# The running sums of squares of the norms added by the vector engine instead of GpSimd

## The chip, the cores and the metric

The kernel runs on one core of one Trainium2 chip. The core has a matrix engine (TensorE, PE in the profile), a vector engine (VectorE, DVE), a scalar engine (ScalarE, ACT), a general engine (GpSimd, POOL) and a queue that issues DMAs (SyncE, SP). The metric is the time of one execution on the device in microseconds (us), as a median of several runs. Outputs are float32.

## The reference, cut to what matters

A two-layer encoder trunk takes 1024 frames of a new stream and 32 frames of a running one, with a model width of 1024. Layer 0 mixes by a gated linear recurrence with 8 heads, layer 1 by sliding-window attention with a sink; each mixer is followed by a gated feed-forward network (FFN) of width 2816. Every sub-layer has a norm in front of it and one behind it, and the result is added to the residual:

```
def rms_norm(x, w):
    xf = x.astype(F32)
    y = xf * lax.rsqrt(jnp.mean(xf * xf, axis=-1, keepdims=True) + NORM_EPS)
    return (y * w.astype(F32)).astype(x.dtype)
...
        x = x + rms_norm(mix, norm_mix_post[layer])
        hf = rms_norm(x, norm_ffn_pre[layer])
        a, b = jnp.split(hf @ w_ffn_in[layer], 2, axis=-1)
        x = x + rms_norm((jax.nn.silu(a) * b) @ w_ffn_out[layer], norm_ffn_post[layer])
```

The change concerns the mean of squares in `rms_norm`: a sum over 1024 features for each of the 1056 frames.

## The kernel before, in words

Activations lie with features on the 128 partitions and frames along the free dimension. The 1056 frames are cut into three blocks, b = 0, 1, 2, of 384, 384 and 288 frames, and the 1024 features into eight slices, k = 0 to 7. Each float32 product on TensorE is made of three products of a high and a low part: weights are split into `wh` (ScalarE casts, L102 or L98) and `wl` (VectorE subtracts, L103 or L99), activations into `xh` (ScalarE, L217 or L220) and `xl` (VectorE, L218 or L221).

A norm needs the sum of squares over all eight slices of a block. `sq_acc` (L176 on) is called once for each slice. For the first slice ScalarE squares straight into the accumulator `acc` (L178). For each of the other seven, ScalarE squares into a scratch tile `tmp` (L181; four buffers that many places share) and the square is added to `acc` (L182). `rnorm` (L184 on) then multiplies a 128x128 matrix of ones with `acc` on TensorE (L188), which sums over the partitions, and VectorE and ScalarE make the inverse square root of it by turns (L163 to L171, with squares and linear steps at L191 and L192).

The sums stand at four places: when the input is loaded (`xload`), behind each mixer's output projection (`outproj`), behind each FFN's last product (`ffn`, L592 adds the product to `mix` and `sq_acc` follows), and in `postnorm`, which scales a slice (L251), adds the residual `xo` that a DMA loaded (L252), splits it into `xh` and `xl`, and sums the squares for the next norm. Eight norms of three blocks with seven adds each give 168 adds.

Around them, the first mixer makes the decays of its recurrence: VectorE makes products of queries and decays (L821 to L851), GpSimd products of keys and decays (L816, L817, L833 to L835, L855 to L858, L941, L942). The second mixer rotates queries and keys: VectorE multiplies (L1129 to L1132), GpSimd combines (L1133, L1134).

The program is written through a framework that fixes, before the run, the order of the instructions of each engine; on the chip each engine takes its instructions in that order and waits at semaphores for what they need. `rnorm` and `rcol` place their small matmuls behind the last dense product that was written so far (`after_dense`), so that their place in TensorE's order is nearly fixed. What one engine has in its queue behind a waiting instruction waits too.

Of the kernel before, what the change touches and what calls it, by code (L numbers as in the profile page):

```python
# [59 lines left out]
def build(nc, tc, I, O):  # L60
    ctx = ExitStack()
    mult, add, sub, mn = ALU.mult, ALU.add, ALU.subtract, ALU.min
# [20 lines left out]
    def tmp(bufs=4):  # L83
        return tp.tile([128, 384], F32, tag="tmp", name="tmp", bufs=bufs)
# [91 lines left out]
    def sq_acc(acc, W, src, first):  # L176
        if first:
            nc.scalar.activation(acc[:, :W], src, AF.Square)  # L178
        else:
            q = tmp()  # L180
            nc.scalar.activation(q[:, :W], src, AF.Square)  # L181
            nc.gpsimd.tensor_tensor(acc[:, :W], acc[:, :W], q[:, :W], add)  # L182

    def rnorm(acc, dst, W, ps=None):  # L184

# [37 lines left out]
    def postnorm(b, mix, acc, w2, xold, wnext, spill, yout, done, more=None, full=None):  # L223
# [25 lines left out]
        for k in range(KT):  # L249
            m = mix[:, k, :]  # L250
            nc.vector.scalar_tensor_tensor(m, m, pcol(w2, k), rb2[:, :W], mult, mult)  # L251
            nc.vector.tensor_tensor(m, m, xos[k][:, :W], add)  # L252
            load()
            if yout is None:
                if full is None:
                    put_x(b, k, m, xs, wnext)
                sq_acc(nacc, W, m, k == 0)
            if k % 2:
                nc.sync.dma_start(dst[:, k - 1:k + 1, :], mix[:, k - 1:k + 1, :])
                if k < KT - 1:  # L260
                    yield
# [23 lines left out]
    def ffn(L, nx, post1, post, wmix, v1, w2, xold, wnext, spill, yout, res):  # L285
# [286 lines left out]
        for b in range(NB):  # L572
            W = BL[b][1]
            pss, un = {}, {}
            accs[b] = newacc(b)

            def first(k):
                if k % 2 == 0:
                    un[0] = units()
                pss[k] = mmps()  # L580
                fmul(pss[k], 2, b, un[0], k % 2, True, False)

            for k in range(4 if b == 0 else 0):
                first(k)
            for k in range(KT):
                if k not in pss:
                    first(k)
                fmul(pss[k], 3, b, units(), 0, False, True)
                if k == 1 and b + 1 < NB:
                    gload(3, b + 1)  # L590
                d = dst(k, b)
                nc.vector.tensor_tensor(d, d, pss[k][:, :W], add)  # L592
                sq_acc(accs[b], W, d, k == 0)
                if b > 0:
                    for _ in range(steps[b][k]):
                        step(b - 1)
# [53 lines left out]
    def outproj(b, arr, pre, w2, xold, wnext, spill, ahead=None):  # L650

        W = BL[b][1]
        oh, ol = os[b]
        mix = mbt[b] = mbs[b].tile([128, KT, 384], F32, tag=mtag(b), name="mixb", bufs=1)
        acc = newacc(b)
        for k in range(KT):
            if k % 2 == 0:
                units = wpair(arr, k // 2, scale=pre)
                if ahead and k < KT - 2:
                    wahead(arr, k // 2 + 1, scale=pre)  # L660
                elif ahead:
                    wahead(*ahead)
            ps = mmps()
            mm_fm(ps, W, units, (k % 2) * 128, lambda q: oh[:, q, :], lambda q: ol[:, q, :])
            nc.scalar.copy(mix[:, k, :W], ps[:, :W])
            sq_acc(acc, W, mix[:, k, :W], k == 0)
            yield

        def done(*r):
            nx[b] = r  # L670

        yield from postnorm(b, mix[:, :, :W], acc, w2, xold[b], wnext, spill[b], None, done,
                            full=("back", "here", None)[b])
# [840 lines left out]
```

## Time and profile before

| what | value |
|---|---|
| median of 3 runs | 2544.05 us (2542.91 to 2549.28) |
| the profiled execution | 2548.6 us |
| its span, first to last instruction | 2546.8 us |
| mean granted TensorE clock in the span | 0.988 |

The durations that the prediction uses come from the profiled execution, which took 2548.6 us; 1.8 us of it lie outside the span. A row of the timeline gives the start in us from the span's start, the length in us, engine, source line, operation, the tile written and those read, shapes, how many instructions the row merges, and in square brackets for how long the engine was idle before and what released it. PEld is TensorE's loading of weights, which runs beside its matmuls.

### The profile page before, as it was taken

The numbers are of one execution on the slowest core, as the hardware profiler recorded it, in microseconds if no ns is written. First come the engines' busy times: TensorE is split into PE (matmuls) and PEld (weight loads), VectorE is DVE, ScalarE is ACT, GpSimd is POOL, SyncE is SP. The second block draws the span as 40 slices with busy tenths as digits, with TensorE's granted clock in tenths as the row PEclk, the third lists the DMA queues.
The fourth block names the chain that finished last, engine by engine and source line by source line (L and its number), as shares of the span: only waits on it lengthen the run. The fifth ranks groups of instructions, "written<-read, shape, count | busy, mean of one in ns | idle before, by whom it ended". The sixth has DMA issues, their size and how long they took to land.

```text
span 2546.8 us, 44040 instructions
## 1 busy us (share of the span) xinstructions
PE 2469.6 (97%) x17124; PEld 2373.7 (93%) x17124; DVE 1722.0 (68%) x3510; ACT 1101.2 (43%) x2395; POOL 457.5 (18%) x644
## 2 busy tenths in 40 slices
PE   7999998999999999999998999999999999999997
PEld 7999998998899999999998997777999999999997
DVE  8788789888776666643467747787776666652456
ACT  6555565666533333341344424565533333342333
POOL 4443444332300000000033321121300000000012
PEclk9999999999999999999999999998999999999998
DMA  5233334343422222242445542332422222252455
GB/s 171 91 101 99 115 110 138 124 135 107 156 72 82 80 77 76 78 166 77 150 158 165 181 128 63 86 120 70 162 80 76 76 76 77 77 177 76 147 168 156
DMA packets 124153, 287.98 MB, mean 113 GB/s; under 512 B 13432, under 2 KB 68632, under 8 KB 123944
## 3 DMA queue, kind: packets, MB, share of 16 engines
q1 hardware_dynamic: 123944, 285.17, 34.9%
q8 instruction: 134, 2.20, 0.3%
q14 instruction: 75, 0.61, 0.1%
HBM read 237.25 MB, written 48.07 MB: 112 GB/s over the span
## 4 chain that ended last, share of the span: by engine, by line
PE 74%; DVE 12%; DMA 5%; ACT 4%; issue 3%; POOL 1%; SPq 0%; POOLq 0%; DVEq 0%; ACTq 0%
PE mm L141 23%; PE mm L507 18%; PE mm L416 14%; PE c L416 6%; PE mm L153 5%; DVE wl L103 2%; PE sc L1272 2%; PE pav L1330 1%; ACT wh L102 1%; PE ptp L1312 1%; DVE wl L99 1%; DMA wst<-in_wfq 1%; DMA xl<-g 1%; DVE mixb L252 1%; DMA xo<-in_x 1%
## 5 line engine op out<-in xcount | busy, mean ns | idle before, releaser
L141 PE MATMUL mm<-xh,wh 128*128 128x384 f32 (+1 forms) x1968 | 632.9, 322 | 11.1 <-ACT xh L220 7.5
L141 PE MATMUL mm<-xh,wl 128*128 128x384 f32 (+1 forms) x1968 | 624.3, 317 | 5.5 <-DVE wl L99 3.0
L141 PE MATMUL mm<-xl,wh 128*128 128x384 f32 (+1 forms) x1968 | 627.1, 319 | 2.0 <-DVE xl L221 1.3
L182 POOL TENSOR_TENSOR acc<-acc,tmp 128x384 f32<-128x384 f32 (+1 forms) x168 | 211.3, 1262 | 1693.7 <-ACT tmp L181 1669.4
L103 DVE TENSOR_TENSOR wl<-wst,wh 128x1024 fp32r<-128x1024 f32 (+1 forms) x301 | 379.3, 1264 | 145.0 <-ACT wh L102 144.4
L102 ACT CAST wh<-wst 128x1024 fp32r<-128x1024 f32 (+1 forms) x301 | 313.6, 1046 | 343.5 <-PE mm L507 198.9
L141 PEld LDWEIGHTS mm<-xh,wh 128*128 128x128 f32 x1968 | 372.8, 190 | 20.9 <-ACT xh L220 7.5
L141 PEld LDWEIGHTS mm<-xh,wl 128*128 128x128 f32 x1968 | 373.0, 190 | 13.8 <-issue 5.6
L141 PEld LDWEIGHTS mm<-xl,wh 128*128 128x128 f32 x1968 | 372.6, 189 | 13.2 <-issue 4.7
L507 PE MATMUL mm<-xh,wl 128*128 128x384 f32 (+1 forms) x768 | 247.1, 322 | 4.7 <-DVE wl L103 4.7
L507 PE MATMUL mm<-xh,wh 128*128 128x384 f32 (+1 forms) x768 | 247.1, 322 | 0.0
L507 PE MATMUL mm<-xl,wh 128*128 128x384 f32 (+1 forms) x768 | 247.0, 322 | 0.0
L153 PE MATMUL mm<-wh,xh 128*128 128x256 f32 (+1 forms) x648 | 189.1, 292 | 3.2 <-DVE tmp L1130 2.2
L153 PE MATMUL mm<-wh,xl 128*128 128x256 f32 (+1 forms) x648 | 185.0, 285 | 0.0
L153 PE MATMUL mm<-wl,xh 128*128 128x256 f32 (+1 forms) x648 | 184.6, 285 | 0.0
L400 ACT CAST sh<-sr 128x512 fp32r<-128x512 f32 x144 | 89.5, 622 | 174.5 <-PE mm L416 146.5
L507 PEld LDWEIGHTS mm<-xh,wl 128*128 128x128 f32 x768 | 144.5, 188 | 5.2 <-DVE wl L103 5.2
L507 PEld LDWEIGHTS mm<-xl,wh 128*128 128x128 f32 x768 | 144.4, 188 | 0.0
L507 PEld LDWEIGHTS mm<-xh,wh 128*128 128x128 f32 x768 | 144.4, 188 | 0.0
L153 PEld LDWEIGHTS mm<-wh,xh 128*128 128x128 f32 (+1 forms) x648 | 119.9, 185 | 6.3 <-DVE tmp L1130 2.4
L153 PEld LDWEIGHTS mm<-wh,xl 128*128 128x128 f32 (+1 forms) x648 | 120.0, 185 | 0.7
L153 PEld LDWEIGHTS mm<-wl,xh 128*128 128x128 f32 (+1 forms) x648 | 119.9, 185 | 0.5
(283 smaller groups left out, 5144.4 us busy)
## 6 DMA issues: line engine op xcount, KB each, us to landing
wst<-in_wfo SPq DMA_DIRECT2D x92, 512.0 KB
wst<-in_wfi SPq DMA_DIRECT2D x88, 512.0 KB
wst<-in_wfq SPq DMA_DIRECT2D x47, 512.0 KB
g<-u SPq DMA_DIRECT2D x72, 192.0 KB
wst<-in_wi SPq DMA_DIRECT2D x24, 512.0 KB
wst<-in_wg SPq DMA_DIRECT2D x24, 512.0 KB
wst<-in_wao SPq DMA_DIRECT2D x24, 512.0 KB
xl<-g SPq DMA_DIRECT2D x32, 384.0 KB
```

The lines of the kernel that those rows point to most:

```text
L99: nc.vector.scalar_tensor_tensor(wl[:, s], st[:, s], pcol(name, k0 + k), wh[:, s].bitcast(F32), mult, sub)
L102: nc.scalar.copy(wh[:, s], st[:, s])
L103: nc.vector.tensor_tensor(wl[:, s], st[:, s], wh[:, s].bitcast(F32), sub)
L141: last_mm[0] = nc.tensor.matmul(ps[:, :W], w, x, start=i == 0, stop=i == n - 1)
L153: last_mm[0] = nc.tensor.matmul(ps[:rows, :256], x, w, start=i == 0, stop=i == n - 1)
L182: nc.gpsimd.tensor_tensor(acc[:, :W], acc[:, :W], q[:, :W], add)
L252: nc.vector.tensor_tensor(m, m, xos[k][:, :W], add)
L400: nc.scalar.copy(h, r)
L416: last_mm[0] = nc.tensor.matmul(ps[:, :384], a, c, start=start and k == i == 0, stop=k == 3 and i == 2, skip_group_check=True)
L507: last_mm[0] = nc.tensor.matmul(ps[:, :W], a, c[:, q, :], start=start and q == i == 0, stop=stop and q == f - 1 and i == 2, skip_group_che ...
L1272: nc.tensor.matmul(pss[pr][:rows, pi, off:off + n], qts[b, g][rsl, pi, qs], kt_[rsl, g, k0:k0 + n], start=pi == 0 and off == lo, stop=samp ...
L1312: nc.tensor.transpose(ptp[:n, hh * rows:hh * rows + rows], P[:rows, hh, off:off + n], ident[:rows, :rows])
```

## The change

In `sq_acc` the add of a square to the accumulator is issued to VectorE (`nc.vector`) and no longer to GpSimd (`nc.gpsimd`). Nothing else is edited. The tiles, the squares on ScalarE and what is computed stay as they are; GpSimd keeps the decays and the rotations.

```
@@ -179,7 +179,7 @@
         else:
             q = tmp()
             nc.scalar.activation(q[:, :W], src, AF.Square)
-            nc.gpsimd.tensor_tensor(acc[:, :W], acc[:, :W], q[:, :W], add)
+            nc.vector.tensor_tensor(acc[:, :W], acc[:, :W], q[:, :W], add)
```

The framework then places the 168 adds in VectorE's order, and moves some other instructions with them. Three places of that order follow; the number in a tile's name tells tiles of one name apart.

The first is the load of block 0 at the start of the program, on VectorE. `xl0_119` is the low part of the input, `acc_120` its sum of squares, `wl_145` and `wl_254` the low parts of weights. Before:

```order
L221 SCALAR_TENSOR_TENSOR xl0_119<-mixb_121,pv_80,xh0_118 128x384
L638 TENSOR_SCALAR oml_96<-lb_95 128x8
L221 SCALAR_TENSOR_TENSOR xl0_119<-mixb_121,pv_80,xh0_118 128x384 x2
L103 TENSOR_TENSOR wl_145<-wst_142,wh_144 128x1024
L221 SCALAR_TENSOR_TENSOR xl0_119<-mixb_121,pv_80,xh0_118 128x384 x4
L103 TENSOR_TENSOR wl_254<-wst_251,wh_253 128x1024
```

and of the change, at the same place:

```order
L221 SCALAR_TENSOR_TENSOR xl0_119<-mixb_121,pv_80,xh0_118 128x384
L638 TENSOR_SCALAR oml_96<-lb_95 128x8
L182 TENSOR_TENSOR acc_120<-acc_120,tmp_128 128x384
L221 SCALAR_TENSOR_TENSOR xl0_119<-mixb_121,pv_80,xh0_118 128x384
L182 TENSOR_TENSOR acc_120<-acc_120,tmp_134 128x384
L221 SCALAR_TENSOR_TENSOR xl0_119<-mixb_121,pv_80,xh0_118 128x384
L182 TENSOR_TENSOR acc_120<-acc_120,tmp_139 128x384
L103 TENSOR_TENSOR wl_145<-wst_142,wh_144 128x1024
```

Each add now stands between the low parts of two slices.

The second is VectorE's order in the first FFN's end, where the `postnorm` of block 0 (`xl0_15464`, sum `acc_15465`) runs beside the last products of block 1 (`mix` from L592, sum `acc_15272`). Before, up to the norm that the sum `acc_15465` feeds (L163 writes `rb0_15730`):

```order
L252 TENSOR_TENSOR mix_13761<-mix_13761,xo_15475 128x384
L251 SCALAR_TENSOR_TENSOR mix_13761<-mix_13761,pv_80,rb2_15395 128x384
L103 TENSOR_TENSOR wl_15680<-wst_15677,wh_15679 128x1024
L218 TENSOR_TENSOR xl0_15464<-mix_13761,xh0_15463 128x384
L252 TENSOR_TENSOR mix_13761<-mix_13761,xo_15532 128x384
L592 TENSOR_TENSOR mix_13761<-mix_13761,mm_15615 128x384
L218 TENSOR_TENSOR xl0_15464<-mix_13761,xh0_15463 128x384
L103 TENSOR_TENSOR wl_15699<-wst_15696,wh_15698 128x1024
L592 TENSOR_TENSOR mix_13761<-mix_13761,mm_15683 128x384
L103 TENSOR_TENSOR wl_15761<-wst_15758,wh_15760 128x1024
L163 TENSOR_SCALAR rb0_15730<-nv_15733 128x384
```

and of the change:

```order
L251 SCALAR_TENSOR_TENSOR mix_13761<-mix_13761,pv_80,rb2_15395 128x384 x2
L182 TENSOR_TENSOR acc_15272<-acc_15272,tmp_15659 128x384
L252 TENSOR_TENSOR mix_13761<-mix_13761,xo_15475 128x384
L252 TENSOR_TENSOR mix_13761<-mix_13761,xo_15532 128x384
L103 TENSOR_TENSOR wl_15680<-wst_15677,wh_15679 128x1024
L218 TENSOR_TENSOR xl0_15464<-mix_13761,xh0_15463 128x384
L182 TENSOR_TENSOR acc_15465<-acc_15465,tmp_15666 128x384
L218 TENSOR_TENSOR xl0_15464<-mix_13761,xh0_15463 128x384
L182 TENSOR_TENSOR acc_15465<-acc_15465,tmp_15673 128x384
L103 TENSOR_TENSOR wl_15699<-wst_15696,wh_15698 128x1024
L592 TENSOR_TENSOR mix_13761<-mix_13761,mm_15683 128x384
L163 TENSOR_SCALAR rb0_15730<-nv_15733 128x384
```

The last two adds of `acc_15465` now stand behind the low parts of the last two slices, and the last `wl` before them moved behind the last residual adds.

The third is GpSimd's order at the end of the first mixer, where a product of keys and decays (L941, tile `K64_8454`) is needed by TensorE's transposes. Before:

```order
L855 TENSOR_TENSOR D64_8459<-D16_8458,SF_8456 128x5
L858 TENSOR_TENSOR K64_8454<-K16_8453,SF_8456 128x5x32
L942 TENSOR_TENSOR D128_8625<-D64_8459 128x2
L182 TENSOR_TENSOR acc_6501<-acc_6501,tmp_8556 128x384
L941 TENSOR_TENSOR K64_8454<-K64_8454,D64_8459 128x2x64
```

and of the change:

```order
L855 TENSOR_TENSOR D64_8459<-D16_8458,SF_8456 128x5
L858 TENSOR_TENSOR K64_8454<-K16_8453,SF_8456 128x5x32
L942 TENSOR_TENSOR D128_8625<-D64_8459 128x2
L941 TENSOR_TENSOR K64_8454<-K64_8454,D64_8459 128x2x64
L1125 TENSOR_TENSOR cosr0_16416<-cosr0_16416,rb0_15730 128x384
```

The add that stood ahead of L941 is gone from GpSimd's order.

More of the change, by code (lines that the diff above doesn't have):

```diff
@@ L181, in sq_acc @@
             nc.scalar.activation(q[:, :W], src, AF.Square)
-            nc.gpsimd.tensor_tensor(acc[:, :W], acc[:, :W], q[:, :W], add)
+            nc.vector.tensor_tensor(acc[:, :W], acc[:, :W], q[:, :W], add)
     def rnorm(acc, dst, W, ps=None):
```

## The prediction

> **What bounds the kernel.** I read the page's busy times first, then busy times by stage, then what TensorE waited for, then the timeline at the longest of these waits.
>
> ```profile
> PE 2469.6 (97%) x17124; PEld 2373.7 (93%) x17124; DVE 1722.0 (68%) x3510; ACT 1101.2 (43%) x2395; POOL 457.5 (18%) x644
> ```
>
> TensorE is busy for 97% of the span, so an edit on other engines can win only what TensorE spends waiting, and the slowed matmuls behind a long wait. The stages (length, then busy us of PE, PEld, DVE, ACT, POOL with instruction counts, granted clock, DMA share, GB/s):
>
> ```profile
> 0.00:700.00 700.00, 667.63 (x5792) 642.11 (x5793) 579.90 (x1604) 409.48 (x1021) 278.11 (x499) 0.99 0.38 123
> 700.00:1250.00 550.00, 548.84 (x3446) 548.61 (x3446) 317.25 (x507) 179.75 (x279) 0.00 (x0) 1.00 0.29 94
> 1305.13:1335.42 30.29, 29.72 (x172) 29.40 (x170) 28.38 (x39) 13.56 (x24) 14.62 (x9) 1.00 0.53 175
> 1337.60:1347.80 10.20, 5.84 (x16) 5.24 (x17) 3.88 (x5) 3.57 (x7) 5.18 (x4) 0.50 0.43 138
> 1805.00:2400.00 595.00, 593.64 (x3717) 592.01 (x3716) 350.69 (x573) 202.10 (x322) 6.24 (x7) 1.00 0.30 97
> ```
>
> Two long stages, 550 and 595 us, hold almost no add and no idle TensorE; nothing will change there. In the first mixer (0 to 700) VectorE is busy for 83%, and in the 30 us from 1305 for 94%. What TensorE waited for (total us, times, longest):
>
> ```profile
> PE mm L188 <- POOL acc L182: 10.1, 3, 7.1
> PE mm L507 <- DVE wl L103: 4.9, 3, 3.0
> PE pt L958 <- POOL K L941: 3.1, 2, 2.1
> PE mm L141 <- DVE wl L99: 3.0, 4, 2.1
> PE mm L141 <- DVE wl L103: 2.5, 3, 1.9
> PE mm L141 <- DVE xl L221: 1.3, 4, 0.5
> ```
>
> The costliest is the wait for the very adds that move, 10.1 us in three waits, 7.1 in one.
>
> **What an add costs before, and what it will cost.** GpSimd's adds by shape, and VectorE's adds of two SBUF tiles of the same shapes (busy us, mean ns):
>
> ```profile
> L182 POOL TENSOR_TENSOR acc<-acc,tmp 128x384 f32<-128x384 f32 x112 | 153.1, 1369 | 1554.6 <-ACT tmp L181 1531.8 <-ACT acc L178 21.2
> L182 POOL TENSOR_TENSOR acc<-acc,tmp 128x288 f32<-128x288 f32 x56 | 58.7, 1049 | 139.0 <-ACT tmp L181 137.6
> L165 DVE TENSOR_TENSOR tmp<-tmp,nv 128x384 f32<-128x384 f32 x16 | 8.9, 554 | 4.6 <-ACT tmp L191 4.4
> L315 DVE TENSOR_TENSOR tmp<-tmp 128x288 f32<-128x288 f32 x44 | 20.1, 457 | 1.0
> ```
>
> So 112 x 0.554 + 56 x 0.457 = 87.6 us go onto VectorE, and its 1722 us would become 1810 if nothing else changed. But the adds on GpSimd slow VectorE already. Rows of the stretch from 1305.1 to 1335.5, in which nine adds run, and single instructions of the same form at moments when GpSimd does not run:
>
> ```profile
> L103 DVE TENSOR_TENSOR wl<-wst,wh 128x1024 fp32r<-128x1024 f32 x6 | 9.7, 1628 | 0.4 <-ACT wh L102 0.4
> L251 DVE SCALAR_TENSOR_TENSOR mix<-mix,pv,rb 128x384 f32<-128x384 f32 x8 | 6.2, 799 | 0.0
> L218 DVE TENSOR_TENSOR xl<-mix,xh 128x384 fp32r<-128x384 f32 x7 | 5.7, 831 | 0.0
> L163 DVE TENSOR_SCALAR rb<-nv 128x384 int32<-128x384 int32 x1 | 1.2, 1178 | 0.0
> ...
> 1299.79 1.23 DVE L103 TENSOR_TENSOR wl<-wst,wh 128x1024 fp32r<-128x1024 f32 x1 [0.81 <-ACT wh L102]
> 1311.01 0.62 DVE L251 SCALAR_TENSOR_TENSOR mix<-mix,pv,rb 128x384 f32<-128x384 f32 x1
> 1335.99 0.56 DVE L218 TENSOR_TENSOR xl<-mix,xh 128x384 fp32r<-128x384 f32 x1
> 1344.17 0.36 DVE L163 TENSOR_SCALAR rb<-nv 128x384 int32<-128x384 int32 x1 [3.11 <-ACT nv L192]
> ```
>
> The excess is 6 x 0.40 + 8 x 0.18 + 7 x 0.27 + 0.82 = 6.6 us, about 0.7 for each of the nine adds. The Trainium skill (SBUF — State Buffer, "Who interferes with whom") says why and says more: a VectorE instruction with two SBUF inputs and a GpSimd instruction that reads SBUF exclude each other, and the second waits for all of the first. By that rule at its worst all 14.62 us of GpSimd's time in the stretch would come back to VectorE; by the rows it is 6.6, and I use the rows.
>
> **Term 1, the 7.1 us wait.** The rows of that place: the last residual add on VectorE and the instruction behind it, the last squares, the adds, and TensorE's last matmul before and first after the wait.
>
> ```profile
> 1334.87 0.55 DVE L252 TENSOR_TENSOR mix<-mix,xo 128x384 f32<-128x384 f32 x1
> 1335.34 0.54 DVE L592 TENSOR_TENSOR mix<-mix,mm 128x384 f32<-128x384 f32 x1
> ...
> 1336.81 1.35 ACT L181 ACTIVATE tmp<-mix 128x384 f32<-128x384 f32 x3
> ...
> 1337.41 5.45 POOL L182 TENSOR_TENSOR acc<-acc,tmp 128x384 f32<-128x384 f32 x4 [2.88 <-ACT tmp L181]
> ...
> 1334.51 0.34 PE L507 MATMUL mm<-xh,wl 128*128 128x384 f32 x1
> 1341.96 1.65 PE L188 MATMUL mm<-acc,ones 128*128 128x384 f32 x2 [7.11 <-POOL acc L182]
> 1345.01 0.52 PE L507 MATMUL mm<-gh,wl 128*128 128x384 f32 x1
> 1345.33 0.52 PE L507 MATMUL mm<-gh,wh 128*128 128x384 f32 x1
> ```
>
> TensorE is done at 1334.85; VectorE ends the last L252 at 1335.42 and GpSimd strings four adds behind it. In the order of the change 11 adds lie between the two L163; started back to back they cost 0.47 each (1334.87 to 1335.34), 5.2 us. Up to the last add of `acc_15465` VectorE also has one L592 and one L218 more than up to its last L252 before, 0.54 + 0.56. So it ends at 1335.42 + 5.2 + 1.1 - 6.6 = 1335.1 without waits for squares. I add 1.2 us for such waits (about two squares of 1.35 / 3 = 0.45, and a start of TensorE): L188 starts at 1336.3 in place of 1341.96, **-5.7**. Bounds: no wait at all, -6.9; each of the 11 adds waiting for a whole square (0.45), 1335.1 + 5.0, only -1.9. Behind the wait the clock row shows 0.50 for 10.2 us, and matmuls start every 0.32 us; by the clock's ratio the 5 us of matmuls from 1342.8 to 1347.8 lose half, 2.5. A wait of 1.5 us should mostly avoid that: **-2.0** (0 to -2.5).
>
> **Terms 2 to 6.** The other stretches in which adds crowd are alike: VectorE spends 0.47 on an add and gets back some 0.6 to 0.7, so it comes out about even or a little ahead. Of the 4.9 us for `wl` at L507 I take **-1.5** (+3 to -4.9); of the 5.5 for `wl` at L141 **-1.5** (+3 to -4). The two shorter waits of L188 (3.0 together): one is in the tail, where GpSimd's add is the last step:
>
> ```profile
> 2530.68 0.79 POOL L182 TENSOR_TENSOR acc<-acc,tmp 128x288 f32<-128x288 f32 x1 [4.05 <-ACT tmp L181]
> ```
>
> VectorE would take 0.45 there, and both together give **-1.0** (0 to -2). At the end of the first mixer an add of 1.61 us holds L941, on which TensorE's transposes wait:
>
> ```profile
> 594.58 1.61 POOL L182 TENSOR_TENSOR acc<-acc,tmp 128x384 f32<-128x384 f32 x1 [14.26 <-ACT tmp L181]
> 596.65 0.55 PE L958 MATMUL pt<-ident,K 128*128 128x128 f32 x3 [1.03 <-POOL K L941]
> ```
>
> Without it: **-0.8** (0 to -1.0). At the start VectorE's L221 is slowed as well:
>
> ```profile
> 7.49 0.62 DVE L221 SCALAR_TENSOR_TENSOR xl<-mixb,pv,xh 128x384 fp32r<-128x384 f32 x1 [1.18 <-ACT xh L220]
> 8.03 0.19 DVE L636 RECIPROCAL e<-e 128x8 f32<-128x8 f32 x1
> 13.60 5.23 DVE L221 SCALAR_TENSOR_TENSOR xl<-mixb,pv,xh 128x384 fp32r<-128x384 f32 x4
> ```
>
> Alone one takes 0.54 from start to start (7.49 to 8.03), so four with adds between them would take 4 x (0.54 + 0.47) = 4.0, not 5.2; the wait of 1.3 for `xl` should shrink: **-1.0** (+0.5 to -1.3).
>
> **Term 7, the cost.** The adds of two stages (GpSimd's busy us in them, count):
>
> ```profile
> 0.00:700.00 700.00, 72.49 (x63) 0.99 0.38 123
> 1400.00:1780.00 380.00, 36.77 (x29) 0.98 0.36 109
> ```
>
> 63 adds stand in the first mixer and 29 between 1400 and 1780. There they are scattered, and each now waits in VectorE's queue for its square; behind it wait the decays, evictions and `wl` that TensorE needs. VectorE has 120 us of idle time in the first 700, which is the cover for 63 x 0.47 = 30 us less the slowing that goes. I take **+3.5** (0 to +16, below).
>
> **Sum.** -7.7 - 1.5 - 1.5 - 1.0 - 0.8 - 1.0 + 3.5 = -10.0 us: 2538.6 against the profiled execution's 2548.6. That one lies 4.5 us above the median of the runs shown, 2544.05, and I carry the difference over: **2534**. With all favourable ends the terms give about -22.
>
> **The rivals.** *The gain is given back* (a third of the chance): VectorE is the bound in the crowded stretches before and after, the adds wait for their squares at the head of its queue, and the 5.7 us fall to 2 or 3 while the `wl` waits grow by as much. For it: 94% busy from 1305. Against: the excess of 6.6 is in the rows. Time: 2544 less 0 to 6, about 2541.
>
> *VectorE becomes the bound of the first mixer*: place 0 to 700, mechanism the in-order queue. The price is 63 adds times a square of about 0.5 us waited out at the head, 32 us in 120 of idle time; if half of it reaches TensorE, +16, and with the 7 to 10 won elsewhere the time is about 2552. It decides from some 0.3 us of wait that reaches TensorE per add. Against it: the squares stand well ahead of the adds, and ScalarE is busy for 58% there. The Trainium skill (Perfetto Trace Analysis, "Optimizing Scalar/DVE Operations") speaks for this rival: where VectorE is saturated, moving work off to GpSimd may pay, which reads as a warning against the way back; it adds that the two share a port, so that it might not. By its first half the 87.6 us would be pure load; no run yet shows VectorE without GpSimd's adds.
>
> *The change does nothing it says*: out, since all 168 adds stand on VectorE in the new order and none on GpSimd.
>
> **How the numbers follow.** My forecast, a gain of 8 to 20 us, has 0.53; the gain given back 0.33; the slower rival 0.14. A measurement of this kernel can tell about 0.3% from no change, 7.6 us, so these are also faster, same and slower. The range from 2523 to 2550 reaches over the second case and to the foot of the third, and leaves out about 0.1 above and somewhat less below.
>
> **What would show it.** The wait of L188 for `acc` near 1335 falls to under 3 us and no stretch with half the clock follows; `wl` of 128x1024 goes back to 1.23 us and L218 to 0.56 wherever GpSimd rests; VectorE's busy time comes to 1730 to 1770 us, not 1810; GpSimd's to about 246. It is wrong if L188 still waits over 5 us, or if new waits for VectorE of a few us each show in the first 700 us; then the adds stall in the queue.

## The result, and the profile after

| what | before | the change |
|---|---|---|
| median, runs side by side | 2545.43 us (2542.91 to 2549.28, 4 runs) | 2527.99 us (2527.16 to 2528.7, 4 runs) |
| ratio | | 0.993, 95% interval 0.9913 to 0.9947 |
| the profiled execution | 2548.6 us | 2527.16 us |
| its span | 2546.8 us | 2525.4 us |

The change is faster by 17.4 us, 0.7%. The line of busy times on the page of the change (busy us, share of the span, instructions):

```profile
PE 2463.1 (98%) x17124; PEld 2370.3 (94%) x17124; DVE 1723.2 (68%) x3678; ACT 1103.5 (44%) x2395; POOL 243.9 (10%) x476
```

VectorE runs 168 instructions more than before and is busy for 1.2 us more (1722.0 before). What the adds themselves take on it, from the groups of the change by line and shape (busy us, mean ns, idle us before them):

```profile
L182 DVE TENSOR_TENSOR acc<-acc,tmp 128x384 f32<-128x384 f32 x112 | 62.2, 555 | 5.7 <-ACT tmp L181 5.5
L182 DVE TENSOR_TENSOR acc<-acc,tmp 128x288 f32<-128x288 f32 x56 | 25.3, 452 | 4.8 <-ACT tmp L181 4.3
```

The adds take 62.2 + 25.3 = 87.5 us, as foreseen to a tenth. Neighbours on VectorE overlap a little (an add is 0.55 us long, and the next instruction starts 0.47 us behind its start, rows below), so busy time rises by less than that. Added up one by one from the two traces, the lengths of the other 3510 instructions, the same ones in both kernels, come to 1910.9 us before and 1839.0 in the change: they became shorter by 71.9 us, 0.43 for each add that left GpSimd. For all 168 adds VectorE waited 10.5 us for squares.

Where the time went is read best between points of the program that both kernels have: matmuls of norms (L188) at 692.70, 1302.84, 1396.33 and 1842.76 us before, and at 685.00, 1293.87, 1377.28 and 1821.78 us of the change. Between two such points both kernels run the same number of matmuls. Busy time of each engine in the five stretches (length; PE, PEld, DVE, ACT, POOL with counts; granted clock; DMA share; GB/s), before:

```profile
0.00:692.70 692.70, 661.12 (x5747) 635.94 (x5748) 574.70 (x1595) 405.89 (x1015) 278.11 (x499) 0.99 0.38 122
692.70:1302.84 610.14, 608.19 (x3797) 607.62 (x3795) 343.71 (x538) 200.25 (x305) 11.03 (x7) 1.00 0.30 97
1302.84:1396.33 93.49, 81.51 (x512) 79.35 (x511) 75.71 (x99) 44.69 (x80) 36.14 (x26) 0.95 0.52 168
1396.33:1842.76 446.43, 432.45 (x2772) 366.48 (x2771) 320.00 (x644) 219.49 (x646) 101.99 (x91) 0.98 0.38 117
1842.76:2546.80 704.04, 686.37 (x4306) 684.28 (x4304) 407.91 (x637) 230.90 (x350) 30.22 (x21) 0.99 0.33 108
```

and of the change:

```profile
0.00:685.00 685.00, 657.44 (x5747) 635.03 (x5748) 570.63 (x1658) 405.90 (x1015) 203.35 (x436) 0.99 0.38 124
685.00:1293.87 608.87, 608.14 (x3797) 607.61 (x3796) 346.74 (x545) 200.26 (x305) 0.00 (x0) 1.00 0.29 98
1293.87:1377.28 83.41, 79.90 (x512) 78.28 (x511) 73.10 (x126) 45.42 (x80) 2.63 (x2) 0.98 0.60 195
1377.28:1821.78 444.50, 431.39 (x2772) 365.08 (x2772) 320.62 (x694) 220.35 (x645) 37.90 (x38) 0.98 0.37 116
1821.78:2525.40 703.62, 686.24 (x4306) 684.35 (x4304) 412.08 (x658) 231.61 (x350) 0.00 (x0) 0.99 0.33 108
```

The stretches became shorter by 7.7, 1.3, 10.1, 1.9 and 0.4 us, 21.4 together (this profiled execution of before lies some 3 us above the median of its runs). Two places carry it: the first mixer, and the end of the first FFN. In the first mixer VectorE does 63 instructions more in 4.1 us less; TensorE waits 27.6 us in place of 31.6, and its 5747 matmuls are busy for 3.7 us less. Fewer of them at half the clock would do that, but a granted clock of 0.99 in both rows doesn't show it. In the third stretch TensorE's waits fall from 12.0 to 3.5 us.

What TensorE waited for in the change, cut to the rows that the prediction names (total us, times, longest):

```profile
...
PE mm L141 <- DVE wl L103: 3.7, 4, 1.5
PE mm L188 <- DVE acc L182: 3.5, 3, 1.6
PE pt L958 <- POOL K L941: 3.4, 1, 3.4
...
PE mm L507 <- DVE wl L103: 2.2, 2, 1.8
```

The wait for the sums fell from 10.1 to 3.5 us. At the place of the old 7.1 us, the timeline of the change shows the last two low parts and adds, and the norm's matmul behind them:

```profile
1293.87 0.81 PE L188 MATMUL mm<-acc,ones 128*128 128x384 f32 x2
...
1325.63 0.55 DVE L182 TENSOR_TENSOR acc<-acc,tmp 128x384 f32<-128x384 f32 x1
1326.10 0.55 DVE L218 TENSOR_TENSOR xl<-mix,xh 128x384 fp32r<-128x384 f32 x1
1326.57 0.55 DVE L182 TENSOR_TENSOR acc<-acc,tmp 128x384 f32<-128x384 f32 x1
1327.17 0.91 PE L188 MATMUL mm<-acc,ones 128*128 128x384 f32 x2 [1.29 <-DVE acc L182]
...
1328.27 0.34 PE L507 MATMUL mm<-gh,wl 128*128 128x384 f32 x1
1328.44 0.33 PE L507 MATMUL mm<-gh,wh 128*128 128x384 f32 x1
1328.62 0.33 PE L507 MATMUL mm<-gl,wh 128*128 128x384 f32 x1
```

TensorE waits 1.29 us there, and a microsecond later the matmuls start every 0.17 us, where before they started every 0.32: the full clock. VectorE goes from instruction to instruction at 0.47 us. In the 31 us ahead of it (1296 to 1327) the groups of VectorE read:

```profile
L103 DVE TENSOR_TENSOR wl<-wst,wh 128x1024 fp32r<-128x1024 f32 x6 | 7.3, 1221 | 1.1 <-ACT wh L102 1.1
L182 DVE TENSOR_TENSOR acc<-acc,tmp 128x384 f32<-128x384 f32 x12 | 6.6, 552 | 0.0
L251 DVE SCALAR_TENSOR_TENSOR mix<-mix,pv,rb 128x384 f32<-128x384 f32 x8 | 4.6, 611 | 0.0
L218 DVE TENSOR_TENSOR xl<-mix,xh 128x384 fp32r<-128x384 f32 x8 | 4.3, 552 | 0.3 <-ACT xh L217 0.3
```

`wl` takes 1.22 us in place of 1.63, L251 0.61 in place of 0.80, L218 0.55 in place of 0.83.

### The profile page after: what moved, and what is told of

Same layout as the page of the kernel before. It is cut to its first block, busy times and chain, and to the rows that moved or that the text cites. A ratio compares the mean times of both kernels' runs of the same rounds, so it can differ in the third digit from the quotient of the medians.

```text
span 2525.4 us, 43811 instructions
## 1 busy us (share of the span) xinstructions
PE 2463.1 (98%) x17124; PEld 2370.3 (94%) x17124; DVE 1723.2 (68%) x3678; ACT 1103.5 (44%) x2395; POOL 243.9 (10%) x476
## 4 chain that ended last, share of the span: by engine, by line
PE 80%; DVE 9%; DMA 4%; ACT 3%; issue 1%; POOL 1%; SPq 0%; DVEq 0%; ACTq 0%; POOLq 0%
PE mm L141 27%; PE mm L507 18%; PE mm L416 15%; PE mm L153 6%; PE c L416 6%; PE sc L1272 2%; DVE wl L103 1%; PE pav L1330 1%; ACT wh L102 1%; PE ptp L1312 1%; DVE wl L99 1%; DVE acc L182 1%; DMA wst<-in_wfo 1%; DMA wst<-in_wfi 1%; DMA wst<-in_wao 1%
## 5 line engine op out<-in xcount | busy, mean ns | idle before, releaser
L141 PE MATMUL mm<-xh,wh 128*128 128x384 f32 (+1 forms) x1968 | 631.2, 321 | 13.6 <-ACT xh L220 8.2
L141 PE MATMUL mm<-xl,wh 128*128 128x384 f32 (+1 forms) x1968 | 626.0, 318 | 2.9 <-DVE xl L1333 2.4
L141 PE MATMUL mm<-xh,wl 128*128 128x384 f32 (+1 forms) x1968 | 623.8, 317 | 3.7 <-DVE wl L103 3.7
L103 DVE TENSOR_TENSOR wl<-wst,wh 128x1024 fp32r<-128x1024 f32 (+1 forms) x301 | 368.2, 1227 | 136.5 <-ACT wh L102 136.0
L141 PEld LDWEIGHTS mm<-xh,wh 128*128 128x128 f32 x1968 | 372.0, 189 | 23.8 <-ACT xh L220 8.7
L141 PEld LDWEIGHTS mm<-xl,wh 128*128 128x128 f32 x1968 | 372.5, 189 | 12.9 <-issue 5.3
L141 PEld LDWEIGHTS mm<-xh,wl 128*128 128x128 f32 x1968 | 373.0, 190 | 10.4 <-DVE wl L103 5.1
L507 PE MATMUL mm<-xh,wl 128*128 128x384 f32 (+1 forms) x768 | 247.4, 322 | 2.2 <-DVE wl L103 2.2
L507 PE MATMUL mm<-xh,wh 128*128 128x384 f32 (+1 forms) x768 | 247.2, 322 | 0.0
L507 PE MATMUL mm<-xl,wh 128*128 128x384 f32 (+1 forms) x768 | 247.2, 322 | 0.0
L507 PEld LDWEIGHTS mm<-xh,wl 128*128 128x128 f32 x768 | 144.9, 189 | 2.7 <-DVE wl L103 2.7
L507 PEld LDWEIGHTS mm<-xl,wh 128*128 128x128 f32 x768 | 144.7, 188 | 0.0
L507 PEld LDWEIGHTS mm<-xh,wh 128*128 128x128 f32 x768 | 144.7, 188 | 0.0
L399 DVE TENSOR_TENSOR sr<-wst 128x512 f32<-128x512 f32 x72 | 49.6, 688 | 74.0 <-DMA wst<-in_wfi 74.0
```

Source lines behind the costliest of these rows:

```text
L103: nc.vector.tensor_tensor(wl[:, s], st[:, s], wh[:, s].bitcast(F32), sub)
L141: last_mm[0] = nc.tensor.matmul(ps[:, :W], w, x, start=i == 0, stop=i == n - 1)
L399: nc.vector.tensor_tensor(r, x, y, op)
L507: last_mm[0] = nc.tensor.matmul(ps[:, :W], a, c[:, q, :], start=start and q == i == 0, stop=stop and q == f - 1 and i == 2, skip_group_che ...
```

## The experiments

Two theories stood against each other. **Slowing**: GpSimd's adds lengthened VectorE's instructions that ran beside them, and that is what went away. **Latency**: an add on GpSimd takes 1.37 us and on VectorE 0.55, so each sum is ready earlier and the waits for it shrink; the slowing is a by-product. A third possibility is that the new order of instructions, not the engine, made the difference in the first mixer. All runs below were made in five rounds beside runs of before on the same chip; on those chips before had medians of 2549.93, 2547.58 and 2550.51 us.

### One place at a time

Before, with only some of the adds on VectorE. `ffn0_only` moves the 42 adds of the first FFN's end and the `postnorm` behind it, `mix0_only` the 63 of the input's load and the first mixer's projection and `postnorm`, `mix1_only` the 42 of the second mixer. The edit of `ffn0_only` against before, cut to the add; the callers hand in the name of the place:

```
-            nc.gpsimd.tensor_tensor(acc[:, :W], acc[:, :W], q[:, :W], add)
+            (nc.vector if place == "ffn0" else nc.gpsimd).tensor_tensor(acc[:, :W], acc[:, :W], q[:, :W], add)
```

> Only the 42 adds at the end of the first FFN and in the postnorm behind it are on VectorE; the other 126 stay on GpSimd. Theory (the gain is local: the 7.1 us wait for the sum, the half clock behind it and the lock on VectorE): 10 to 13 us below the kernel before, since the norm matmuls of the two traces stand 9.0 us apart at 1303 and 21.0 us apart at 1440 us; L188 waits under 2 us near 1335. Rival (the new order of the other engines, spread over the program, makes the gain): at most 4 us below.

> Only the 63 adds of the input load and of the first mixer's projection and postnorm are on VectorE. The two traces stand 7.7 us apart at the end of this stage. Theory (VectorE gains more from the missing GpSimd adds than the adds cost): 5 to 9 us below the kernel before. Rival (the prediction's cost term: VectorE is 83% busy here and the adds stall its queue): 0 to 4 us above it, the 7.7 us being what the profiled execution of before was slower than its median.

> Only the 42 adds of the second mixer's projection and postnorm are on VectorE. The two traces move apart by 4.8 us up to 1733 us and together again by 5.3 us up to 1843. Theory (local gain and loss in balance): within 3 us of the kernel before. Rival (the attention stage gains as the other stages do): 4 to 6 us below.

| run | median us | ratio to before (95%) | difference |
|---|---|---|---|
| `ffn0_only` | 2542.11 | 0.9969 (0.9957 to 0.9982) | -7.8 |
| `mix0_only` | 2538.16 | 0.9956 (0.9941 to 0.9972) | -11.8 |
| `mix1_only` | 2551.73 | 1.0008 (0.9998 to 1.0018) | none to be told |

The three differences of the medians, -7.8 - 11.8 + 1.8, make -17.8; the change has -17.4. (The 21 adds of the second FFN's end were not run alone.) Within the intervals, which reach 3 to 4 us to each side for the first two, the gain is the sum of what is won at each place. `ffn0_only` falls between its two expectations (10 to 13, and at most 4), `mix0_only` wins more than the 5 to 9 that were expected, and `mix1_only` is as expected. The row of the long wait in `mix0_only`, whose adds in the FFN stay on GpSimd:

```profile
1334.93 1.01 PE L188 MATMUL mm<-acc,ones 128*128 128x384 f32 x1 [7.11 <-POOL acc L182]
```

The wait is untouched, and the gain is from elsewhere. In `ffn0_only` the same matmul waits 1.40 us:

```profile
1337.79 0.59 PE L188 MATMUL mm<-acc,ones 128*128 128x384 f32 x1 [1.40 <-DVE acc L182]
```

So a good share of the gain comes from the part of the program where I had put the cost. Which of the two shares is the larger, the medians don't tell: their intervals, 5 to 11 us and 7 to 15, overlap.

### The change with GpSimd's adds put back beside it

`shadow` keeps the change, and lets GpSimd add every used square to itself, a result that nothing reads. The sum's chain is as short as in the change, and the order of the engines nearly the same. Against the change:

```
-            nc.vector.tensor_tensor(acc[:, :W], acc[:, :W], q[:, :W], add)
+            nc.vector.tensor_tensor(acc[:, :W], acc[:, :W], q[:, :W], add); nc.gpsimd.tensor_tensor(q[:, :W], q[:, :W], q[:, :W], add)
```

> All 168 adds on VectorE as in the change, and behind each GpSimd adds the used square to itself, so that GpSimd reads SBUF as often as before while nothing waits for its result but the scratch buffer. Theory (each engine's SBUF reads hold up the other): VectorE's busy time rises from 1723 to 1780 or more, the low parts of 128x1024 weights slow down again in the crowded stretches, and the time goes back by 10 us or more, to 2538 or above, worse than before if VectorE bounds the crowded stretches. Rival (the gain is that the sum is ready sooner, and GpSimd's queue is free): VectorE's time matters little and the kernel stays at 2527 to 2532.

It took 2560.84 us, ratio 1.0047 (1.0031 to 1.0062): 10.9 us slower than before, and some 29 slower than the change (0.993 of 2549.93 is 2532). Its busy times:

```profile
PE 2471.8 (97%) x17124; PEld 2374.0 (93%) x17124; DVE 1777.1 (69%) x3678; ACT 1103.1 (43%) x2395; POOL 428.9 (17%) x644
```

The same 3678 instructions of VectorE take 53.9 us more than in the change, a little under the 1780 us that had been expected. The timeline of `shadow` near 1330 shows single ones:

```profile
1329.25 1.08 POOL L182 TENSOR_TENSOR tmp<-tmp 128x384 f32<-128x384 f32 x1 [0.49 <-DVE acc L182]
1329.56 1.84 DVE L103 TENSOR_TENSOR wl<-wst,wh 128x1024 fp32r<-128x1024 f32 x1
...
1332.27 1.21 DVE L103 TENSOR_TENSOR wl<-wst,wh 128x1024 fp32r<-128x1024 f32 x1
1332.43 1.74 POOL L182 TENSOR_TENSOR tmp<-tmp 128x384 f32<-128x384 f32 x1 [2.10 <-DVE acc L182]
...
1339.30 1.07 POOL L182 TENSOR_TENSOR tmp<-tmp 128x384 f32<-128x384 f32 x1 [2.57 <-DVE acc L182]
1339.62 1.18 DVE L182 TENSOR_TENSOR acc<-acc,tmp 128x384 f32<-128x384 f32 x1
1340.87 0.83 POOL L182 TENSOR_TENSOR tmp<-tmp 128x384 f32<-128x384 f32 x1 [0.49 <-DVE acc L182]
```

Whoever starts second is longer. `wl` that starts behind GpSimd's add takes 1.84 us; `wl` that starts 0.16 us ahead of one takes 1.21, and then it is GpSimd's add that takes 1.74, where the last row has 0.83. The whole trace of before says the same when its instructions are counted. A `wl` of 128x1024 takes 1.22 us on average with GpSimd idle (193 of them), 1.22 when an instruction of GpSimd starts after it (46), and 1.45, at most 2.04, when it starts while one of GpSimd runs (60). For `xl` of L218 (128x384) the three are 0.55, 0.55 and 1.05 (32, 4 and 12). An L592 of 128x288, which reads one of its two inputs from PSUM (the memory that TensorE writes to) and not from SBUF (where the other tiles lie), takes 0.45 with GpSimd idle and 0.45 behind it (12 and 4).

The norm's matmul at that place waits again, though its adds are on VectorE:

```profile
1348.37 1.01 PE L188 MATMUL mm<-acc,ones 128*128 128x384 f32 x1 [5.66 <-DVE acc L182]
...
PE mm L188 <- DVE acc L182: 11.7, 5, 5.7
...
PE mm L141 <- DVE wl L103: 8.8, 6, 3.6
```

11.7 us for the sums, more than before's 10.1, and 8.8 for `wl` at L141, where the change has 3.7. Latency as the main cause is out: a short chain without relief of VectorE is worth less than nothing. The 10.9 us above before are what 168 adds cost VectorE while GpSimd keeps running as many, less whatever the shorter chain wins; this run doesn't part the two. It prices the slowing a little low, since an add of a tile to itself is shorter on GpSimd (0.83 us with VectorE idle) than an add of before (0.99 to 1.02).

### Is it reading, or merely GpSimd being busy?

`shadow_set` has the same tiles at the same places, but GpSimd fills them with zeros, so it writes and reads nothing. Against `shadow`, cut to GpSimd's part:

```
-            nc.gpsimd.tensor_tensor(q[:, :W], q[:, :W], q[:, :W], add)
+            nc.gpsimd.memset(q[:, :W], 0.0)
```

> The change, and behind each of the 168 adds GpSimd fills the used square with zeros: it writes the same tiles at the same places of the order as the full shadow, which added them to themselves, but reads nothing, and takes some 0.3 us in place of 1.2. The scratch tile is held in the same way as in the full shadow. Theory that the two engines shut each other out when both read: the time is that of the change, ratio 0.993 (0.992 to 0.995), L182 on the vector engine stays near 0.5 us. Rival, the full shadow's cost came from the scratch tile given back later and the other names in the order: ratio near 1.003. Rival, any access of GpSimd slows the vector engine for as long as it lasts: a quarter of the 28.6 us, ratio about 0.996.

It took 2529.53 us, ratio 0.9929 (0.9913 to 0.9944): the change's time. The busy line:

```profile
PE 2467.6 (97%) x17124; PEld 2371.8 (94%) x17124; DVE 1722.8 (68%) x3678; ACT 1103.1 (44%) x2395; POOL 311.4 (12%) x644
```

GpSimd spends 67.5 us on 168 fills, and VectorE's busy time, 1722.8, is that of the change. The fills are shorter than the adds, but that doesn't explain it: in `shadow` 185.0 us more of GpSimd brought 53.9 more of VectorE, and at that rate 67.5 would bring 20, not none. A scratch tile that another engine must give back, or other names in the order, cost nothing here; what costs is an add on GpSimd, which reads, and not a fill. The Trainium skill (SBUF — State Buffer, "Who interferes with whom") states this: a VectorE instruction with two SBUF inputs contends with GpSimd instructions that read SBUF, and not with those that only write it. This pair of runs agrees.

### The slowing in the first mixer alone

`shadow_mix0` is `shadow` with GpSimd's adds in the load and the first mixer only, 63 of them. Against the change, cut to the add:

```
-            nc.vector.tensor_tensor(acc[:, :W], acc[:, :W], q[:, :W], add)
+            nc.vector.tensor_tensor(acc[:, :W], acc[:, :W], q[:, :W], add); ((place in ("load", "mix0")) and nc.gpsimd.tensor_tensor(q[:, :W], q[:, :W], q[:, :W], add))
```

> The change, and behind each of the 63 adds of the input's load and the first mixer GpSimd adds the used square to itself (a tile that nothing reads after): the vector engine's order stays that of the change, and GpSimd again runs 63 adds of the old size beside it, in that part only. This prices how much of the first mixer's gain (mix0_only, -11.2 us) is the slowing of the vector engine by GpSimd's adds and how much the other order of the instructions. Slowing: the full shadow cost 28.6 us against the change for 168 adds, 0.17 each, so 63 cost about 11 us, and the time is about 2543 where before is 2550 and the change 2532 (ratio to before 0.997, range 0.995 to 0.999). Order: the gain stays, the cost is under 3 us, ratio 0.993 to 0.994. The latter part of the program (from 700 us) goes as in the change in both.

It took 2544.68 us, ratio 0.9988 (0.9977 to 1.0): about 15 us more than the change (0.0058 of 2548; with both intervals, 10 to 20). The stretch of the first mixer in its trace, up to the same L188 as in the tables above:

```profile
0.00:700.74 700.74, 662.43 (x5746) 636.29 (x5747) 596.66 (x1658) 405.60 (x1015) 273.52 (x499) 0.99 0.38 121
```

Against the change's 685.00 us with the same 1658 instructions of VectorE, VectorE is busy for 26.0 us more and the stretch is 15.7 us longer. GpSimd's adds stand right behind VectorE's here, and not at the moments of before, so this prices the same thing at a somewhat different place. The traces of the other runs, read between the same L188, put a price on both sides; each number is one profiled execution:

| run | first mixer, up to that L188, us | end of the first FFN (the third stretch), us |
|---|---|---|
| before | 692.70 | 93.49 |
| `mix1_only` | 693.24 | 92.75 |
| `ffn0_only` | 694.64 | 83.13 |
| `mix0_only` | 686.48 | 91.43 |
| the change | 685.00 | 83.41 |
| `shadow_set` | 686.08 | 83.34 |
| `rope_dve` (below) | 688.34 | 83.84 |
| `shadow_mix0` | 700.74 | 83.25 |
| `shadow` | 701.77 | 93.76 |

In the first mixer the three traces with the adds on GpSimd have 693.5 us on average, the four with them on VectorE 686.5, and the two that have adds on both 701.3. So the slowing that went is worth some 15 us there, more than the 11 expected, the adds on VectorE cost some 8, and some 7 are won; the interval of `mix0_only`'s -11.8, which is from medians, just reaches this. At the FFN's end `shadow` gives all of the 10 us back. Another order of instructions isn't needed to explain the gain: `shadow_mix0` and `shadow` keep the change's order on VectorE but for 15 of 3678 places, and lose it.

### What else GpSimd might give up

If VectorE gets back about what it pays, other GpSimd work should move too. `rope_dve` moves the combining of the rotations (L1133, L1134), `k941_dve` the last step of the keys' decays (L941, L942), `both_dve` both, and `all_dve` all arithmetic that GpSimd has left (by `KE = nc.vector` and L1125 besides). The edit of `both_dve` against the change, cut:

```
-        nc.gpsimd.tensor_tensor(a[:, 0, :W], a[:, 0, :W], t1[:, :W], sub)
-        nc.gpsimd.tensor_tensor(a[:, 1, :W], a[:, 1, :W], t2[:, :W], add)
+        nc.vector.tensor_tensor(a[:, 0, :W], a[:, 0, :W], t1[:, :W], sub)
+        nc.vector.tensor_tensor(a[:, 1, :W], a[:, 1, :W], t2[:, :W], add)
...
-            KE.tensor_tensor(Kh[:, :, 0], Kh[:, :, 0], Dh[:, :, 1:2].broadcast_to([128, n, 64]), mult)
-            KE.tensor_tensor(D128[:, :n], Dh[:, :, 0], Dh[:, :, 1], mult)
+            V.tensor_tensor(Kh[:, :, 0], Kh[:, :, 0], Dh[:, :, 1:2].broadcast_to([128, n, 64]), mult)
+            V.tensor_tensor(D128[:, :n], Dh[:, :, 0], Dh[:, :, 1], mult)
```

> The change, and also the two combining steps of the rotations (L1133, L1134; 30 instructions, 30 us on GpSimd) on the vector engine. A candidate for a version faster than the change. Theory from the place runs (the 42 adds of the second mixer on the vector engine moved nothing there, ratio 1.0008): about 14 us more on the vector engine less the slowing that goes, 70 % busy there, so within 0.1 % of the change, ratio 0.992 to 0.994. Rival: the rotations' chain gets shorter by 0.5 us a step and the slowing of L1130 and L1132 goes, gain of 3 to 6 us more, ratio 0.991. Rival: the vector engine's queue becomes the wait for the attention's keys, ratio 0.995 or more.

> The change, and also the last step of the keys' decays in the first mixer (L941, L942; 48 instructions, 21 us on GpSimd) on the vector engine, which leaves the rest of the decays on GpSimd. TensorE waits for L941 3.4 us in the change. A candidate for a version faster than the change. Theory as for the first mixer's adds (the cost is paid by the slowing that goes): the wait falls to about 1 us, ratio 0.991 to 0.993. Rival: the vector engine is 83 % busy there and L941 at the head of its queue waits for GpSimd's L858, so that evictions behind it are late: ratio 0.995 or more.

> The change with the rotations' combining (L1133, L1134) and the last step of the keys' decays (L941, L942) on the vector engine: the two candidates together. Measured against before, the change has 0.993, the rotations 0.9912, the decays' last step 0.9899. Theory that the gains stand at separate places (second and first mixer) and add: 0.9929 - 0.0017 - 0.0030, so 0.988 (0.987 to 0.9895). Rival, what they win is the same time (the spread of the order's chance effects): no better than the best of the two, 0.990 to 0.991.

> The change with every remaining arithmetic instruction of GpSimd on the vector engine too (all of the keys' decays, L816 to L942, the rotations, L1125), so that the two never meet; GpSimd keeps only the fills. How far does it carry that the vector engine gets back what it pays? In the first mixer of the change GpSimd has 203 us and the vector engine 583 of 700. The instructions are small (6 to 192 elements a partition), some 370, at 0.2 to 0.4 us each on the vector engine, 90 to 110 us, and the slowing that goes is at most about half of that. Theory A, the vector engine still has cover (583 + 50 of 700, 90 %): near the change or better, 0.990 to 0.995. Theory B, the first mixer becomes bound by the vector engine's queue: 10 to 40 us more than the two candidates together, 0.995 to 1.005. I hold B for the likelier.

| run | median us | ratio to before (95%) |
|---|---|---|
| the change | 2527.99 | 0.993 (0.9913 to 0.9947) |
| `rope_dve` | 2525.11 | 0.9912 (0.9897 to 0.9927) |
| `k941_dve` | 2521.7 | 0.9899 (0.9883 to 0.9914) |
| `both_dve` | 2517.41 | 0.9873 (0.9854 to 0.9892) |
| `all_dve` | 2529.29 | 0.9916 (0.9899 to 0.9933) |

`both_dve` beats both kernels: 33 us faster than before, and its interval lies below the change's. Its two parts add up as expected (0.988). `rope_dve` alone can't be told from the change; its median lies nearer to the rival's 0.991 than to the theory's 0.992 to 0.994. `k941_dve` wins more than the 0.991 to 0.993 that were expected, and its first mixer is 677.8 us long where the change has 685.0. In its waits the 3.4 us for L941 fall to 1.0, as expected, and that for `xl` at L1026, 4.4 in the change, is down to 2.1:

```profile
PE pt L958 <- DVE K L941: 1.0, 1, 1.0
PE pgt L1026 <- DVE xl L1029: 2.1, 2, 1.2
```

`all_dve` gives back what `both_dve` won. In its first 700 us, against 583.42 on VectorE and 203.35 on GpSimd in the change:

```profile
0.00:700.00 700.00, 669.37 (x5807) 643.35 (x5808) 618.94 (x2079) 410.34 (x1024) 3.56 (x28) 0.99 0.40 123
```

200 us of GpSimd's work cost VectorE only 35.5, yet the first mixer, up to the L188 of the table, is 690.4 us long where `both_dve` has 676.9. TensorE waits longer for the low parts of weights, 11.2 us against the change's 3.7:

```profile
PE mm L141 <- DVE wl L103: 11.2, 9, 4.1
```

Of its two expectations the first, near the change, has the right number; the second was right that it loses to `both_dve` (by 0.0043, 11 us), and wrong that it loses to the change. It was the second that had been held for the likelier.

## Why the prediction was right, and where it was not

The direction and the range held: 2528 lies in 2523 to 2550, on the better side of the 2534. The price of the long wait held by its mechanism. That the whole sum came so near is in part luck: one term had the wrong sign, and the range, 27 us wide, had room for it. Step by step:

- **The 7.1 us wait (term 1, -5.7).** Right in mechanism and size. From the norm's matmul ahead of it to this one, before has 1341.96 - 1302.84 = 39.12 us and the change 1327.17 - 1293.87 = 33.30: -5.8. The half clock behind it (-2.0): the 512 matmuls of this stretch take 1.6 us less. The rows show no matmul at half the clock behind the 1.29 us wait.
- **`wl` at L507 (term 2, -1.5).** From 4.9 to 2.2, -2.7. With term 1 the stretch was to win 9.2 us; it won 10.1.
- **`wl` at L141 (term 3, -1.5).** From 5.5 to 3.7, all of it now behind L103: -1.8.
- **The shorter waits of L188 (term 4, -1.0).** From 3.0 to 3.5 - 1.3 = 2.2: -0.8.
- **L941 near 596 (term 5, -0.8).** The wait is gone, but nothing was won: in its place TensorE waits 1.35 us for an evicted `at` (row below), and the other wait for L941, near 53 us, grew from 2.1 to 3.4.

```profile
594.01 0.49 PE L1006 MATMUL po<-vt,at 128*128 128x128 f32 x2 [1.35 <-ACT at L897]
```

- **The start (term 6, -1.0).** The first norm's matmul starts at 18.11 in place of 20.93 us, -2.8; my bound was -1.3. In `shadow` it starts at 20.43, so it was the slowing that held it. By the next norm's matmul only 0.9 of it is left (112.74 in place of 113.61), which is the size of the term.
- **The cost in the two mixers (term 7, +3.5).** This is the term that was wrong, in its sign. In the second mixer no difference can be told (1.0008), but not because nothing happens there. From the L188 at 1396.33 to the one at 1732.88, three traces with these adds on GpSimd (before, `mix0_only`, `ffn0_only`) have 336.6, 336.4 and 336.3 us, and the change and `mix1_only` 329.3 and 331.8; from there to the one at 1842.76 the three have 109.9, 105.7 and 105.0, and the two 115.2 and 114.9. A gain and a cost cancel. In the first mixer I let the adds wait for their squares at the head of VectorE's queue; the 63 adds waited 3.8 us in all (their row below). And I left the relief of VectorE out of TensorE's time there, since VectorE had idle time to cover both. The runs put the relief at about 15 us and the adds at about 8.

```profile
L182 DVE TENSOR_TENSOR acc<-acc,tmp 128x384 f32<-128x384 f32 (+1 forms) x63 | 32.7, 527 | 3.8 <-ACT tmp L181 3.4
```

The step behind it was to treat the 17% idle time of VectorE as cover. If it had covered a cost, it would also have hidden the relief, and `mix0_only` would have shown nothing. It shows 7 to 12 us. The sign was asked of the adds alone; it should have been asked of both sides. Added up from the traces, the 63 adds are 33.2 us long and VectorE's other instructions in that stretch went from 674.6 to 642.6, 32.0 less: about even on VectorE. That an even exchange won 7 us means that a microsecond of slowing held TensorE up more often than a microsecond of an add; why it did, no run shows.

VectorE's busy time was to come to 1730 to 1770 us and came to 1723.2, for two reasons. The slowing, which I knew from one crowded stretch, was nearly as large where the adds are scattered: 0.51 us for each add in the first mixer, 0.54 in the third stretch, where the crowd is (81.6 to 67.4 us over 26 adds), and 0.40 in the fourth (356.2 to 335.8 over 51). And the 87.6 that I added are whole lengths, which overlap with their neighbours. The rule at its worst, that all of GpSimd's time comes back to VectorE, was not reached: 71.9 us of the 153.1 + 58.7 = 211.8 that the adds took on GpSimd, 0.34.

The rival that the gain is given back is out: no wait for `wl` grew by as much as L188's fell (the largest growth is L103 at L141, 2.5 to 3.7). The rival that VectorE becomes the bound of the first mixer asked for 0.3 us of wait per add and got 3.8 us for 63; even the 8 us that the adds cost there are only 0.13 for each. The Trainium skill (Perfetto Trace Analysis, "Optimizing Scalar/DVE Operations"), which spoke for it, was borne out by its second half, that work moved between the two engines might not help; `all_dve` shows where its first half begins to hold: with VectorE busy for 619 us of 700, the first mixer lost more by the added instructions than the end of the slowing gave.

What stays open: which single delays of VectorE in the first mixer reach TensorE. One stall of before, 2.3 us for `kT` (L960) at 125 us, whose copy stood in ScalarE's queue behind steps of a norm, is not among the change's long waits, and no run took it apart from the rest.

## What to carry to other kernels

Before you price a move from GpSimd to VectorE, compare the same VectorE instruction beside GpSimd and alone (here 1.63 against 1.22 us, 0.83 against 0.55); if the excess per GpSimd instruction is about the price on VectorE, the move is free on VectorE's busy time, and what TensorE had waited for the shortened instructions can be won. Idle time of an engine covers nothing by itself: at 83% busy, VectorE's shortened instructions still won 7 to 12 us. Move in parts and stop early: 168 adds and 78 further instructions won 33 us, and the rest of GpSimd's arithmetic gave a third of it back.

## What was not expected of the hardware

TensorE's clock falls to half behind some short waits and not behind longer ones. Take the 3.4 us that follow two waits in before, one of 3.04 us (1386.62) and one of 1.88 us (1794.61). Their rows come first, then the busy times in those windows, where the third number from the end is the granted clock:

```profile
1386.62 0.40 PE L507 MATMUL mm<-xh,wl 128*128 128x288 f32 x1 [3.04 <-DVE wl L103]
1794.61 0.40 PE L141 MATMUL mm<-xh,wl 128*128 128x288 f32 x1 [1.88 <-DVE wl L103]
```

```profile
1386.62:1390.02 3.40, 3.40 (x25) 3.40 (x26) 3.40 (x5) 1.49 (x3) 2.04 (x2) 1.00 0.95 294
1794.61:1798.01 3.40, 3.40 (x15) 3.40 (x16) 2.48 (x2) 2.23 (x5) 3.24 (x4) 0.56 0.83 270
```

Behind the longer wait 25 matmuls ran at full clock, behind the shorter 15 at 0.56. In the change, no half clock followed the 1.29 us wait of L188, and a clock of 0.63 over 3.4 us followed its 1.57 us wait at 2509.88. So the length of a wait alone doesn't tell what it costs, and "a wait of 1.5 us should mostly avoid that" was luck as much as reason.
